# Where the operands of the matrix multiplications start in SBUF: weights at 0, moving activations at 192, stationary activations at 0, modulo 256 bytes

## The chip, the core and the metric

One core of a Trainium2 chip runs the whole program. The metric is the time of one execution on the device in microseconds (us). A core has TensorE (PE; its weight loads are listed apart, as PEld), VectorE (DVE), ScalarE (ACT), GpSimd (POOL) and SyncE (SP), which here issues the weight transfers.

## The reference

Two transformer blocks work on one sequence of 256 tokens of width 1024, all in float32.

```python
# first block
z = rms_norm(x, g_mix) @ w_in
x = x + (gate0 * y_pool + gate1 * y_nsa + gate2 * y_mem) @ w_o      # pooling, sparse attention, memory attention
x = x + peer_ffn(rms_norm(x, g_ffn), w_q, sub_keys, u, v)           # 16384 one-neuron experts, top 16 of each of 8 heads
x = rms_norm(x, g_final)
# second block, two layers: the mixer is mla in the first, fox in the second
h = h + 0.5 * swiglu(rms_norm(h), w_in, w_out)                      # d_ff 2816
h = h + mixer(rms_norm(h))
h = h + 0.5 * swiglu(rms_norm(h), w_in, w_out)
h = h + sigmoid(rms_norm(h) @ w_gate) * (p @ w_proj)
return rms_norm(h)
```

The kernel computes the product with all 16384 experts densely: `peer_u` is a 1024 x 16384 projection, `peer_v` a 16384 x 1024 one, and the top-16 gates are a mostly zero factor between them.

## The kernel before, in words

Every large weight comes in units of 128 partitions x 1024 columns (512 KB). `unit` (L243) gives each unit one DMA into a `raw` buffer (three of them), then a rounding copy on ACT into `hi` (L262, type float32r) and the remainder `lo = raw - hi` on DVE or POOL (L263). Activations are split in the same way. `mm3` (L279) makes one product of three matmuls from a stationary pair L and a moving pair R: L281 multiplies the hi of both, L282 the hi of L with the lo of R, L283 the lo of L with the hi of R.

There are two forms. In `ws_chunk` the weights are stationary (128 columns) and the activations X move past them, 256 tokens at a time: 8 steps of `mm3`, 24 matmuls for a unit. It is used for 20 units of `w_ws`, 16 of `peer_q`, 128 of `peer_u`, 176 of `ffn_in` and 16 of `fox_qk`: 356 units, 8544 matmuls. In the other form (`proj`, `go`, `cols_xs`) the activations are stationary and 512 columns of weights move: 12 matmuls for a unit. `peer_v` has 128 such units (1536 matmuls), `ffn_out` 88 (1056).

A matmul reads its moving operand from SBUF while the stationary operand of the next one is loaded, also from SBUF. Both run along the free dimension in every partition, so what can differ between two buffers is the byte address at which they start in the partition. The allocator rounds tiles up to 32 bytes and lays the tiles of a pool one behind the other. In the program before, the `raw` buffers begin at byte 18528 of the partition, the tiles that live across stages (`h0`, `h1`, `hThi`, ...) at 63936, and the tiles of each stage at 93952 = 367 x 256. This gives, modulo 256 bytes:

- `whi` (four buffers of 1032 floats = 4128 bytes): 192, 224, 0, 32; `wlo`: 64, 96, 128, 160. They are used as the pairs (192, 64), (224, 128), (0, 96), (32, 160).
- the `wx` places, where units go while attention buffers are free (the tiles of `qT`, `kT`, `v`, `Ohi`, `Olo` in the second block): 128 for hi and lo alike; the places in `U`, in the second half of `peer_v`: 0 for both.
- `hThi` and `hTlo`, the activations that move in most `ws_chunk` calls: 192; `Xhi` and `Xlo` of the second block (moving in `fox_qk`): 0.
- stationary activations: `W` and the upper part of `U` in `peer_v` 0, `ah` in `ffn_out` 128, `t2hi`/`t2lo` 32, `y4`/`Mt` 96, `Ohi`/`Olo` 128.

Two units are named below by their buffers: the unit that runs from 505.3 to 508.2 us lies in the pair (192, 64), and the one from 508.2 to 511.05 us in the pair (0, 96). The unit from 1509.8 to 1512.5 us lies in a `wx` place (128, 128). All three have X at 192.

The program is one fixed order for each engine: PE's order follows the Python loops and `weave`. `order` (L220) turns the four pairs and the places round. In the first part of `peer_u` the routing of tokens to experts (`routing`, L1020) runs on DVE beside it, and POOL makes every `lo`.

Of the kernel before, what the change touches and what calls it, by code (L numbers as in the profile page):

```python
# [9 lines left out]
F32 = mybir.dt.float32  # L10
F32R = mybir.dt.float32r
BF16 = mybir.dt.bfloat16
I32 = mybir.dt.int32
# [9 lines left out]
WU = 1032  # L23
# [115 lines left out]
N_G = 99  # L139
# [64 lines left out]
class Prog:  # L204
# [38 lines left out]
    def unit(self, src, w=1024, parts=1):  # L243

        nc = self.nc
        raw = self.strm.tile([128, WU], F32, name="raw", bufs=3)[:, :w]
        cuts = [slice(i * w // parts, (i + 1) * w // parts) for i in range(parts)]
        for c in cuts:
            nc.sync.dma_start(raw[:, c], src[:, c])
        self.n_unit += 1  # L250

        i = next(i for i in self.order if i < 0 or i in self.slots and w <= 1024)
        self.order.remove(i)
        self.order.append(i)
        if i >= 0:
            hi, lo = [v[:, :w] for v in self.slots[i]()]
        else:
            hi = self.strm.tile([128, WU], F32R, name="whi", bufs=4)[:, :w]
            lo = self.strm.tile([128, WU], F32R, name="wlo", bufs=4)[:, :w]
        e = nc.gpsimd if self.pool_lo and self.n_unit % self.pool_lo == 0 else nc.vector  # L260
        for c in cuts:
            nc.scalar.activation(hi[:, c], raw[:, c], AF.Copy)  # L262
            e.tensor_tensor(lo[:, c], raw[:, c], f32(hi[:, c]), op=OP.subtract)  # L263
        return hi, lo
# [147 lines left out]
    def run(self):  # L412
        nc, tc, a = self.nc, self.tc, self.a
        self.ones = self.const.tile([128, 1], F32, name="ones")
        nc.vector.memset(self.ones, 1.0)
        self.mhalf = self.const.tile([128, 1], F32, name="mhalf")

        nc.scalar.activation(self.mhalf, self.ones, AF.Copy, scale=-0.5)
        self.gc = self.const.tile([128, N_G], F32, name="gc")
        nc.sync.dma_start(self.gc, a["gcols"])  # L420
        i_ = self.const.tile([128, 128], I32, name="iota_i")
        nc.gpsimd.iota(i_, pattern=[[1, 128]], base=0, channel_multiplier=0)
        self.ident = self.const.tile([128, 128], F32, name="ident")
        nc.sync.dma_start(self.ident, a["c_ident"])
        self.io = self.const.tile([128, 128], F32, name="io")
        nc.vector.tensor_copy(self.io, i_)
        self.h = [self.res.tile([128, 1024], F32, name=f"h{t}") for t in range(2)]
        if WARM:

            z = self.h[0][:, :256].bitcast(BF16)  # L430
            nc.vector.memset(self.h[0][:, :256], 0.0)
            ps = self.mm()
            for _ in range(WARM):
                nc.tensor.matmul(ps, z[:, :128], z, start=True, stop=True)
        with ExitStack() as s:
            self.block1(s)
        if self.stop <= 1:
            return
        with ExitStack() as s:
            self.peer(s)  # L440
        if self.stop <= 2:
            return
        with ExitStack() as s:
            self.block2(s)
# [5 lines left out]
    def block1(self, s):  # L450
        nc, tc, a = self.nc, self.tc, self.a
        b1 = s.enter_context(tc.tile_pool(name="b1", bufs=1))
        self.junk = b1.tile([128, 1024], BF16, name="junk")

        turn = [0]
# [34 lines left out]
        X = N.X  # L490
# [38 lines left out]
        for t in range(2):  # L529
            n = 7 if t == 0 else 15  # L530
            ps = self.mm()
            for c in range(n):
                o = 128 - t * 128 + 16 * c + 31
# [43 lines left out]
        for c in "kv":  # L577
            w = b1.tile([128, 16, 64], F32, name="wcmp" + c, tag="pooled" if c == "k" else "uu")
# [75 lines left out]
        def cmp_scores(t):  # L654
            yield on("Ck", "sig", "q")
            ps = self.mm()
            for i in range(8):
                r, gp = divmod(i, 2)
                self.m32(ps[:, i * 32:(i + 1) * 32], qT[:, i, t * 128:(t + 1) * 128],
                         kcbd[:, gp].rearrange("p a b -> p (a b)"))  # L660
            sc = b1.tile([128, 16, 15], F32, name="sc")
            pr = b1.tile([128, 16, 32], F32, name="prc", tag="pr", bufs=4)
            st = b1.tile([128, 4, 16], F32, name="stc")
            nc.gpsimd.memset(pr, 0.0)
            nc.vector.tensor_tensor(sc.rearrange("p (g r) b -> p r g b", r=4),
                                    ps[:, :256].rearrange("p (r g b) -> p r g b", r=4, b=16)[:, :, :, :15],
                                    biasc[:, t].rearrange("p (g r) b -> p r g b", r=4), op=OP.add)
            nc.vector.tensor_reduce(st[:, 0], sc, axis=AX.X, op=OP.max)
            nc.vector.tensor_tensor(sc, sc, st[:, 0, :, None].to_broadcast([128, 16, 15]), op=OP.subtract)
            nc.scalar.activation(sc, sc, AF.Exp)  # L670
            nc.vector.tensor_reduce(st[:, 1], sc, axis=AX.X, op=OP.add)
            nc.vector.reciprocal(st[:, 2], st[:, 1])
            nc.vector.tensor_tensor(st[:, 3], st[:, 2], sig[:, t, 0], op=OP.mult)
            if t == 0:
                nc.vector.tensor_scalar(st[:, 3], st[:, 3], has, None, op0=OP.mult)
            nc.vector.tensor_tensor(pr[:, :, :15], sc, st[:, 3, :, None].to_broadcast([128, 16, 15]), op=OP.mult)
            yield 5.0
            pt = self.mm()
            for g in range(4):
                self.tpose(pt[:, g * 128:(g + 1) * 128], pr[:, 4 * g:4 * g + 4].rearrange("p r b -> p (r b)"))  # L680
            nc.scalar.activation(pct[:, t, :, ::-1], pt.rearrange("p (g q) -> p g q", g=4), AF.Copy)
            flag.add(f"pc{t}")
# [141 lines left out]

        kx = b1.tile([128, 4, 256], F32, name="kx")
        qx = b1.tile([128, 4, 256], F32, name="qx")
        vx = b1.tile([128, 2, 512], F32, name="vx")

        def memory():
            Nm = Norm(self, b1, self.gc[:, G_MEM:], x=(b1.tile([128, 8, 256], F32R, name="t2hi"),  # L830
# [125 lines left out]
    def peer(self, s):  # L956
        nc, tc, a = self.nc, self.tc, self.a
# [6 lines left out]
        X = N2.X  # L964
# [31 lines left out]
        for hp in range(16):  # L996
# [12 lines left out]
            if 4 <= hp < 12:  # L1009
                k = hp - 4  # L1010
# [4 lines left out]
            nc.scalar.activation(X[0][:, k], Hn[:, k], AF.Copy)  # L1015
            nc.vector.tensor_tensor(X[1][:, k], Hn[:, k], f32(X[0][:, k]), op=OP.subtract)  # L1016

        rt = self.res.tile([128, 1024], F32, name="rt")[:, :768].rearrange("p (i t) -> p i t", i=3)

        def routing(t):  # L1020
            o = 18432 if t == 0 else 30720
# [118 lines left out]
        for ip in range(64):  # L1140
# [4 lines left out]
            n = prog["tok"]  # L1145
# [28 lines left out]
                         tuple(u[j][:, h * 512:(h + 1) * 512] for j in range(2)), i == 0, i == 127)  # L1174

        gfin = self.res.tile([128, 1024], F32, name="gfin", tag="rt")
        gg = self.res.tile([128, 8], F32, name="gg")
        nc.vector.tensor_tensor(gg, self.gc[:, G_FIN:G_FIN + 8], self.gc[:, G_F2:G_F2 + 8], op=OP.mult)
        for i in range(128):
            if i == 64:  # L1180
# [17 lines left out]
        self.N3 = N3 = Norm(self, self.res, gg, x=self.hT(),  # L1198
                                 y=lambda: view(next(ys), 512))
        ss = N3.ss  # L1200
        r1 = self.res.tile([128, 2], F32, name="r1")

        self.junk = view(12288, 512, BF16)
        s2 = self.res.tile([128, 2, 2], F32, name="s2")
# [31 lines left out]
    def block2(self, s):  # L1236
        nc, tc, a = self.nc, self.tc, self.a
# [13 lines left out]
        turn = [0]  # L1251

        def next_norm(g):
            turn[0] ^= 1
            X = (tuple(b2.tile([128, 8, 256], F32R, name="X" + c) for c in ("hi", "lo")) if turn[0] else self.hT())
            return Norm(self, b2, self.gc[:, g:], x=X, y=ny)

        def res_stage(N, scale=None):
# [507 lines left out]
```

## Time and profile before

| | us |
|---|---|
| median of 3 runs | 2249.47 (2247.63 to 2249.92) |
| the profiled execution | 2250.61 |
| its span, first to last instruction | 2248.8 |
| PE busy | 2194.7 (98%) |
| DVE busy | 1505.9 (67%) |
| ACT busy | 1094.4 (49%) |
| POOL busy | 164.3 (7%) |
| DMA, mean busy share of 16 engines | about 50% |

The page gives one execution. "mean ns" of a matmul runs from its start to its modelled end, and neighbours overlap: PE starts the next one before that end. How often PE starts one is read from a stretch in which it does nothing else: length through count. Times inside the trace are counted from the first instruction.

### The profile page before, as it was taken

The numbers are of one execution on the slowest core, as the hardware profiler recorded it, in microseconds if no ns is written. First come the engines' busy times: TensorE is split into PE (matmuls) and PEld (weight loads), VectorE is DVE, ScalarE is ACT, GpSimd is POOL, SyncE is SP. The second block draws the span as 40 slices with busy tenths as digits, with TensorE's granted clock in tenths as the row PEclk, the third lists the DMA queues.
The fourth block names the chain that finished last, engine by engine and source line by source line (L and its number), as shares of the span: only waits on it lengthen the run. The fifth ranks groups of instructions, "written<-read, shape, count | busy, mean of one in ns | idle before, by whom it ended". The sixth has DMA issues, their size and how long they took to land. (4 is left out here: it accounts for less than half of the span.)

```text
span 2248.8 us, 37085 instructions
## 1 busy us (share of the span) xinstructions
PE 2194.7 (98%) x14402; PEld 1980.8 (88%) x14402; DVE 1505.9 (67%) x3071; ACT 1094.4 (49%) x1739; POOL 164.3 (7%) x141
## 2 busy tenths in 40 slices
PE   6999999999999999999999999999999999999998
PEld 5987788899999998888887999889998999989996
DVE  6656557998888985566565754865556655675555
ACT  3356544455444444455544543654445544554445
POOL 5000000284000000000001000100001000000000
PEclk7999999999999999999999999999999999999999
DMA  5632255455444456556554754445554653555553
GB/s 183 202 132 76 85 179 195 132 187 168 148 148 150 150 174 204 190 190 216 190 193 133 232 190 147 135 149 189 187 169 149 224 189 124 187 170 187 187 183 104
DMA packets 105171, 378.18 MB, mean 168 GB/s; under 512 B 12089, under 2 KB 12273, under 8 KB 104738
## 3 DMA queue, kind: packets, MB, share of 16 engines
q1 hardware_dynamic: 102832, 369.24, 50.0%
q0 software_dynamic: 1920, 6.37, 0.9%
q8 instruction: 113, 1.85, 0.3%
q14 instruction: 64, 0.52, 0.1%
q10 hardware_dynamic: 242, 0.20, 0.0%
HBM read 373.62 MB, written 2.14 MB: 167 GB/s over the span
## 5 line engine op out<-in xcount | busy, mean ns | idle before, releaser
L262 ACT ACTIVATE whi<-raw 128x1024 fp32r<-128x1024 f32 (+3 forms) x527 | 551.2, 1047 | 534.2 <-PE mm L282 347.6
L263 DVE TENSOR_TENSOR wlo<-raw,whi 128x1024 fp32r<-128x1024 f32 (+3 forms) x493 | 598.4, 1217 | 285.7 <-ACT whi L262 284.9
L281 PE MATMUL mm<-hThi,whi 128*128 128x256 f32 x2080 | 593.6, 286 | 22.9 <-ACT hThi L304 13.8
L282 PE MATMUL mm<-hTlo,whi 128*128 128x256 f32 x2080 | 589.9, 284 | 4.0 <-DVE hTlo L1016 2.7
L283 PE MATMUL mm<-hThi,wlo 128*128 128x256 f32 x2080 | 586.8, 282 | 1.2 <-DVE wlo L263 1.2
L281 PEld LDWEIGHTS mm<-hThi,whi 128*128 128x128 f32 x2080 | 394.6, 190 | 28.6 <-ACT hThi L304 14.0
L282 PEld LDWEIGHTS mm<-hTlo,whi 128*128 128x128 f32 x2080 | 396.2, 191 | 8.1 <-DVE hTlo L1016 2.9
L283 PEld LDWEIGHTS mm<-hThi,wlo 128*128 128x128 f32 x2080 | 395.4, 190 | 2.1 <-DVE wlo L263 2.1
L263 DVE TENSOR_TENSOR wx<-raw,wx 128x1024 fp32r<-128x1024 f32 x140 | 173.4, 1239 | 107.1 <-ACT wx L262 107.0
L262 ACT ACTIVATE wx<-raw 128x1024 fp32r<-128x1024 f32 x140 | 147.7, 1056 | 135.7 <-PE mm L283 95.2
L281 PE MATMUL mm<-hThi,wx 128*128 128x256 f32 x640 | 179.3, 281 | 2.4 <-ACT hThi L164 2.4
L282 PE MATMUL mm<-hTlo,wx 128*128 128x256 f32 x640 | 179.5, 281 | 0.3 <-DVE hTlo L165 0.3
L283 PE MATMUL mm<-hThi,wx 128*128 128x256 f32 x640 | 179.2, 280 | 0.0
L281 PEld LDWEIGHTS mm<-hThi,wx 128*128 128x128 f32 x640 | 120.6, 189 | 4.1 <-ACT hThi L164 2.8
L282 PEld LDWEIGHTS mm<-hTlo,wx 128*128 128x128 f32 x640 | 120.7, 189 | 1.7 <-issue 0.5
L283 PEld LDWEIGHTS mm<-hThi,wx 128*128 128x128 f32 x640 | 121.0, 189 | 0.0
L1103 DVE TENSOR_SCALAR h<-io,rt 128x128 f32<-128x128 f32 x256 | 93.7, 366 | 22.2 <-PE mm L273 21.9
L281 PE MATMUL acc<-whi,W 128*128 128x512 f32 x256 | 101.0, 395 | 0.0
L283 PE MATMUL acc<-whi,W 128*128 128x512 f32 x256 | 101.0, 394 | 0.0
L282 PE MATMUL acc<-wlo,W 128*128 128x512 f32 x256 | 100.8, 394 | 0.0
L263 POOL TENSOR_TENSOR wlo<-raw,whi 128x1024 fp32r<-128x1024 f32 x34 | 85.1, 2510 | 68.0 <-ACT whi L262 66.2
L1304 ACT ACTIVATE ah<-sg 128x256 fp32r<-128x256 f32 x88 | 36.6, 416 | 97.8 <-DVE sg L1301 97.8
(497 smaller groups left out, 4053.9 us busy)
## 6 DMA issues: line engine op xcount, KB each, us to landing
raw<-in_ffn_in SPq DMA_DIRECT2D x176, 512.0 KB, 3.7
raw<-in_peer_u SPq DMA_DIRECT2D x128, 512.0 KB, 3.8
raw<-in_peer_v SPq DMA_DIRECT2D x128, 512.0 KB, 3.5
raw<-in_ffn_out SPq DMA_DIRECT2D x88, 512.0 KB, 3.6
raw<-in_w_mrg SPq DMA_DIRECT2D x24, 512.0 KB, 3.5
raw<-in_w_ws SPq DMA_DIRECT2D x19, 512.0 KB, 4.2
raw<-in_w_peer_q SPq DMA_DIRECT2D x16, 512.0 KB, 4.3
raw<-in_ple_g SPq DMA_DIRECT2D x16, 512.0 KB, 3.5
```

The source lines that it names most:

```text
L262: nc.scalar.activation(hi[:, c], raw[:, c], AF.Copy)
L263: e.tensor_tensor(lo[:, c], raw[:, c], f32(hi[:, c]), op=OP.subtract)
L281: m(ps, L[0], R[0], start=first, stop=False, skip_group_check=True)
L282: m(ps, L[0], R[1], start=False, stop=False, skip_group_check=True)
L283: m(ps, L[1], R[0], start=False, stop=last, skip_group_check=True)
L1103: nc.vector.tensor_scalar(A[:, j], self.io, i1, g, op0=OP.is_equal, op1=OP.mult)
L1304: nc.scalar.activation(hi, sg, AF.Copy)
```

## The change

It changes where tiles start and what they are padded to. No arithmetic changes, and `mm3`, its callers and the order of the units stay.

- `unit`: the separate tiles `whi` and `wlo` become one tile `w2` of 2112 floats (8448 bytes, 33 x 256), four buffers as before; hi starts at float 0, lo at float 1024 (at 1056 for the wide units of `fox_v`).
- the constants `iota_i` and `io` (512 bytes each) leave the constant pool; `io` now lies in free columns of `rt`, and `iota` on POOL with its copy on DVE is issued in `peer` just ahead of the routing. `gc` is padded from 99 to 115 columns.
- `gg` is taken first in its pool and padded to 192 bytes, `r1` padded to 64; the first block's `stc` and `vx` are padded; `Xhi` and `Xlo` become tiles of 2112 and 2144 floats of which columns 48 to 2096 are used.

```diff
@@ unit
-            hi = self.strm.tile([128, WU], F32R, name="whi", bufs=4)[:, :w]
-            lo = self.strm.tile([128, WU], F32R, name="wlo", bufs=4)[:, :w]
+            pair = self.strm.tile([128, 2112], F32R, name="w2", bufs=4)
+            o = 1024 if w <= 1024 else 1056
+            hi, lo = pair[:, :w], pair[:, o:o + w]
@@ run
-        self.gc = self.const.tile([128, N_G], F32, name="gc")
-        nc.sync.dma_start(self.gc, a["gcols"])
-        i_ = self.const.tile([128, 128], I32, name="iota_i")
-        nc.gpsimd.iota(i_, pattern=[[1, 128]], base=0, channel_multiplier=0)
+
+        self.gg = self.res.tile([128, 48], F32, name="gg")[:, :8]
+        self.h = [self.res.tile([128, 1024], F32, name=f"h{t}") for t in range(2)]
+        self.gc = self.const.tile([128, N_G + 16], F32, name="gc")
+        nc.sync.dma_start(self.gc[:, :N_G], a["gcols"])
         self.ident = self.const.tile([128, 128], F32, name="ident")
         nc.sync.dma_start(self.ident, a["c_ident"])
-        self.io = self.const.tile([128, 128], F32, name="io")
-        nc.vector.tensor_copy(self.io, i_)
-        self.h = [self.res.tile([128, 1024], F32, name=f"h{t}") for t in range(2)]
@@ block1
-            st = b1.tile([128, 4, 16], F32, name="stc")
+            st = b1.tile([128, 112], F32, name="stc")[:, :64].rearrange("p (a b) -> p a b", a=4)
...
-        vx = b1.tile([128, 2, 512], F32, name="vx")
+        vx = b1.tile([128, 1080], F32, name="vx")[:, :1024].rearrange("p (t d) -> p t d", t=2)
@@ peer
-        rt = self.res.tile([128, 1024], F32, name="rt")[:, :768].rearrange("p (i t) -> p i t", i=3)
+        rt = self.res.tile([128, 1024], F32, name="rt")
+        self.io = rt[:, 768:896]
+        rt = rt[:, :768].rearrange("p (i t) -> p i t", i=3)
+        i_ = view(20480 - 128, 128, I32)
+        nc.gpsimd.iota(i_, pattern=[[1, 128]], base=0, channel_multiplier=0)
+        nc.vector.tensor_copy(self.io, i_)
...
-        gg = self.res.tile([128, 8], F32, name="gg")
+        gg = self.gg
...
-        r1 = self.res.tile([128, 2], F32, name="r1")
+        r1 = self.res.tile([128, 16], F32, name="r1")[:, :2]
@@ block2
-            X = (tuple(b2.tile([128, 8, 256], F32R, name="X" + c) for c in ("hi", "lo")) if turn[0] else self.hT())
+            X = (tuple(b2.tile([128, n], F32R, name="X" + c)[:, 48:2096].rearrange("p (k t) -> p k t", k=8)
+                       for c, n in (("hi", 2112), ("lo", 2144))) if turn[0] else self.hT())
```

## Rows read from the trace of the kernel before

**Rows 1.** The page: its span and PE's line.

```profile
span 2248.8 us, 37085 instructions
PE 2194.7 (98%) x14402; PEld 1980.8 (88%) x14402; DVE 1505.9 (67%) x3071; ACT 1094.4 (49%) x1739; POOL 164.3 (7%) x141
```

**Rows 2.** PE's waits, longest in total first: total us, times, longest.

```profile
PE mm L281 <- ACT hThi L304: 13.8, 1, 13.8
PE mm L281 <- ACT hThi L164: 8.6, 4, 2.6
```

**Rows 3.** Windows: busy us and instructions of each engine, clock, DMA share, GB/s.

```profile
core 0: us, PE busy (x) PEld busy (x) DVE busy (x) ACT busy (x) POOL busy (x), PEclk, DMA share, GB/s
...
500.00:535.00 35.00, 35.00 (x297) 35.00 (x296) 34.96 (x59) 18.11 (x21) 27.02 (x12) 1.00 0.53 176
560.00:820.00 260.00, 260.00 (x2223) 260.00 (x2222) 227.31 (x661) 117.66 (x203) 0.00 (x0) 1.00 0.46 151
870.00:1035.00 165.00, 165.00 (x712) 133.28 (x711) 99.70 (x126) 83.44 (x128) 0.00 (x0) 1.00 0.57 190
...
1260.00:1380.00 120.00, 119.84 (x855) 112.44 (x854) 73.10 (x90) 57.13 (x76) 0.00 (x0) 1.00 0.62 202
1509.77:1512.49 2.72, 2.72 (x26) 2.72 (x25) 2.39 (x3) 1.06 (x1) 0.00 (x0) 1.00 0.66 229
```

**Rows 4.** Groups by line within 500 to 535 us: count, busy us, mean ns.

```profile
L281 PE MATMUL mm<-hThi,whi 128*128 128x256 f32 x99 | 27.8, 281 | 0.0
```

**Rows 5.** Groups by line within 870 to 1035 us.

```profile
L282 PE MATMUL acc<-wlo,W 128*128 128x512 f32 x237 | 93.3, 394 | 0.0
```

**Rows 6.** Single lines, 509.28 to 511.04 us: count, ns min/median/max, first and last start.

```profile
L281 PE MATMUL mm<-hThi,whi x5: 277/277/277, 509.3 to 510.7; 128*128 128x256 f32 x5
L282 PE MATMUL mm<-hTlo,whi x6: 285/285/286, 509.0 to 510.8; 128*128 128x256 f32 x6
L283 PE MATMUL mm<-hThi,wlo x6: 278/279/279, 509.2 to 510.9; 128*128 128x256 f32 x6
```

**Rows 7.** The same for one line, 506.45 to 508.2 us.

```profile
L281 PE MATMUL mm<-hThi,whi x5: 278/282/285, 506.4 to 507.9; 128*128 128x256 f32 x5
```

**Rows 8.** The same for one line, 1509.9 to 1512.25 us.

```profile
L281 PE MATMUL mm<-hThi,wx x8: 276/276/276, 1509.8 to 1512.1; 128*128 128x256 f32 x8
```

**Rows 9.** The same for one line, 508.22 to 508.5 us.

```profile
L281 PE MATMUL mm<-hThi,whi x1: 287/287/287, 508.2 to 508.2; 128*128 128x256 f32 x1
```

**Rows 10.** Groups by line within 1260 to 1380 us.

```profile
L282 PE MATMUL mm<-hTlo,wx 128*128 128x256 f32 x120 | 33.5, 279 | 0.0
```

**Rows 11.** Single lines, 1060 to 1185 us, units in the places of U.

```profile
L281 PE MATMUL acc<-U x78: 389/389/398, 1064.9 to 1184.4; 128*128 128x512 f32 x78
L282 PE MATMUL acc<-U x78: 387/389/389, 1065.1 to 1184.6; 128*128 128x512 f32 x78
```

**Rows 12.** Groups by line over the whole span.

```profile
L282 PE MATMUL mm<-hTlo,wx 128*128 128x256 f32 x640 | 179.5, 281 | 0.3 <-DVE hTlo L165 0.3
L282 PE MATMUL acc<-wx,ah 128*128 128x512 f32 x184 | 71.9, 391 | 0.0
L282 PE MATMUL acc<-wlo,ah 128*128 128x512 f32 x168 | 66.5, 396 | 0.0
L283 PE MATMUL acc<-whi,y 128*128 128x512 f32 x32 | 13.0, 407 | 0.0
```

**Rows 13.** Groups by line within 10 to 100 us.

```profile
L281 PE MATMUL mm<-hThi,whi 128*128 128x256 f32 x125 | 36.4, 291 | 13.8 <-ACT hThi L304 13.8
```

**Rows 14.** POOL by line, 424 to 520 us, and the timeline at the start.

```profile
L263 POOL TENSOR_TENSOR wlo<-raw,whi 128x1024 fp32r<-128x1024 f32 x29 | 73.0, 2525 | 66.8 <-ACT whi L262 65.1 <-PE mm L281 1.5
0.84 0.24 POOL L422 IOTA iota_i<- 128x128 int32 x1 [0.40 <-POOLq L1758]
```

**Rows 15.** Timelines of DVE and PE where the second routing ends.

```profile
531.28 2.47 DVE L1104 TENSOR_SCALAR h<-io,rt 128x128 f32<-128x128 f32 x1
539.51 0.49 PE L287 MATMUL mm<-ident,R 128*128 128x128 f32 x3
```

## The prediction

> **What bounds the kernel now.** I read the page first: of the span of 2248.8 us PE is busy 2194.7 [rows 1], and PE's waits are short: the longest is 13.8 us, once, at the start, and the next group 8.6 us in total [rows 2]. So the time is what PE's stream takes. Then I read stretches in which PE does one thing [rows 3]. From 870 to 1035 us it starts 712 matmuls of 512 columns, two of them reaching in from the left: 165 / 710 = 232.4 ns each; their mean duration is 394 ns [rows 5]. From 500 to 535 us, matmuls of 256 columns: 35 / 295 = 118.6 ns, with durations of 281 ns and a little over [rows 4]. In both, start to start is the duration less 162 to 163 ns, so a duration in ns tells the pace of one matmul to a nanosecond: pace = duration - 162.5.
>
> Next, what the pace depends on. In the unit from 508.2 to 511.05 us (weights at 0 and 96, X at 192) the three lines settle at 277, 285 and 279 ns, the same at nearly every step [rows 6]. While L281 runs, hi is loaded once more (at 0, for L282); while L282 runs, lo (at 96, for L283); while L283 runs, hi (at 0). So a moving operand that starts 192 bytes after the one being loaded, modulo 256, goes with 277 to 279 ns (114.5 to 116.5 of pace), one 96 after it with 285 (122.5). The unit before it (192 and 64) wavers between 278 and 285 on one line [rows 7]. The fastest pace is in the unit at 1509.8 us: 276 ns at every step [rows 8], and as a check 2.72 us for 24 starts, 113.3 ns [rows 3]. Other units in such places have 279 on average [rows 10]. For 512 columns the best rows are in U, where weights and stationary operand both start at 0: 389 ns [rows 11], against 394 beside it. So the pace of one and the same matmul differs by 2 to 8% with where its operands lie and how it falls in with its neighbours, and the clock is 1.00 in all these stretches, its upper level of 2.4 GHz.
>
> **The change part by part.** Where things end up: the constant pool loses 1024 bytes and gains 64, so raw begins at 17568 and the pairs at 17568 + 3 x 4128 = 29952 = 117 x 256. Each is 33 x 256 long: hi and lo at 0 in all four. They end at 63744, gg takes 192, and h0 begins at 63936 as before: hThi and hTlo stay at 192. In the second block Xhi and Xlo get 192 by their 48 columns, and the two are 640 bytes longer, which moves ah, wx, Ohi, Olo from 128 to 0. In the first, the pads move t2 and y4 to 0. So 256-column matmuls get the distance 192 throughout, and 512-column ones 0, except where X itself is stationary (gates, fox_v, mla_down, ple_g: distance 64; I give these nothing).
>
> 256 columns, weights in the four pairs: of 8544 matmuls in 356 units 3 x 640 = 1920 are in wx [rows 12], which leaves 6624. In the first 100 us PE waits for its transfers; the 3 x 125 there [rows 13] I count at nothing. 6250 remain, at 281.3 ns. For the new pace the bounds are 276, the lowest row [rows 8], and 281.3, no gain; I take 277, which the distance 192 shows in the row nearest to the new state: hi loaded after hi, both at 0 [rows 6]. 6250 x 4.3 ns = 26.9 us. In wx: 1920 x (279.3 - 277) = 4.4 us.
>
> 512 columns: peer_v has 64 units x 12 = 768 matmuls with W at 394.3, which go to the 389.7 of the rows in U: 3.5 us. Of its second 64 units about 37 (four of seven places) lie in the pairs: 444 x 4.3 = 1.9 us. In ffn_out the pairs have 396 to 397 (504 matmuls), the places wx some 393 (552) although both their operands are at 128, distance 0 as well: entering from 256-column work costs something that the layout may leave. I take 391.5 for both: 504 x 5.5 = 2.8 and 552 x 1.5 = 0.8 us. Products with t2, y4, Mt, O stationary (some 528, 395 in clean stretches; single groups are at 407 with their waits [rows 12]): 528 x 3.5 = 1.8 us. Sum 10.8 us; the bounds are 0 and, at 389.5 everywhere, 15.
>
> What lies beside it. While POOL makes every lo, one takes 2525 ns [rows 14], and a unit of PE goes from 24 x 118.6 = 2.85 to 2.75 us: it still fits, with 0.2 us to spare. DVE is full until about 534 us (34.96 of 35 in [rows 3]). By 531 us it has left the routing for the gating (L1104), and PE reads the routing's result at 539.5 [rows 15], so PE could come 8 us earlier; at the new pace it comes 3 us earlier. In the gating that follows DVE is busy 227 of 260 us [rows 3], 87%; at the new pace about 90%. Since little is to spare in the routing, I take 3 us off for it. If that cover were gone altogether, the gain of peer_u (3072 x 4.3 = 13 us) would go. ACT and DMA are at 62% or less.
>
> The moved constants: iota takes 0.24 us on POOL [rows 14]; the copy on DVE I put at 0.3, by the other 128-column DVE operations in these rows without their waits. They now stand ahead of the routing on engines that wait for that stage's first tiles; nothing is queued behind them there but the routing, which starts 8 us ahead of need by the same rows. Between -0.3 (the start loses them) and +0.5 us: 0. The merged tile: hi's buffer now comes free with lo's, one matmul later (0.12 us) and four units ahead of need: 0. Pads: 0.
>
> The sum: 26.9 + 4.4 + 10.8 - 3 = 39.1 us. Against the profiled execution, 2250.6 - 39.1 = 2211.5; that one is 1.1 us above the median of the runs, so 2210 for the median.
>
> The Trainium skill, in "TensorE: Matmul & The Clock Gate", step 1 of Part 2, speaks against the change: PE has two independent SBUF read ports, and loading the next weights takes no read bandwidth from the running matmul. By that, layout would be worth nothing and the time stays 2249. The trace does not agree as far as the pace goes: 277 and 285 ns alternate in one unit whose matmuls differ in nothing but the operands' place [rows 6]. What is shared the trace does not tell; rival 2 reaches the same time from rows of this kernel.
>
> **The rivals.**
> 1. The pace is a matter of phase more than of distance. For: the same addresses (192, 128, 128) give 276 in one unit [rows 8] and 279 on average [rows 10]; and 277 + 285 + 279 makes 841, near 3 x 279 = 837, as if the credit of one line were paid by the next. Against: 277 stands in five steps running, always on the same line. Then all 256-column work settles at 279.3: 6250 x 2.0 = 12.5, plus 10.8 for the 512-column work: 23 us, 2226 us; with half of the 512-column gain and none for wx 2231.
> 2. Layout does nothing by itself: what looks like place is which engine writes beside it. By it each unit keeps its pace and the time is 2249. For: units in the pair (192, 64) waver [rows 7], which a fixed place would not. Against: [rows 6] and [rows 11], steady over whole units.
> 3. Slower: a bad phase that keeps itself up. The first L281 of the unit in [rows 6] has the favoured distance and takes 287 ns, 124.5 of pace [rows 9]. With every unit alike there is no neighbour of another class to knock the stream out of it. If all of it enters so and stays: 6250 x 5.7 + 1920 x 7.7 = 50 us, less 10.8: 2289. It is slower from the point where the mean of the 256-column work, now 280.8 over the two kinds, rises by more than 10.8 us / 8170 = 1.3 ns, above 282.1. Against: in that unit it is gone after three steps.
> 4. Another engine sets the end in peer_u: 13 - 3 = 10 us are lost, 2220.
>
> **How the numbers follow.** Forecast (a mean of 276 to 278 for 256 columns: 2202 to 2218) 0.70; rival 1 0.15; rival 2 0.06; rival 3 0.05; rival 4 0.04. The predicted time is 2210. The lower end: at 276 everywhere the 256-column term is 33.1 + 6.3 = 39.4, and the 512-column one at most 15: with the 3 us off, 51 us, 2198; I take 2199. The upper end takes in rivals 1 and 4: 2232. A measurement of this kernel tells about 0.2%, 4.5 us, from no change. Faster by more than that: 0.70 + 0.15 + 0.04 = 0.89; within it: rival 2, 0.06; slower: rival 3, 0.05.
>
> **What would show it.** In the changed profile L281, L282 and L283 of the 256-column groups should all have a mean near 277, without the 285 on L282; 870 to 1035 us (now earlier) should have about 390 for all three lines with W; windows of pure 256-column work should give 114.5 ns a matmul. PE's waits should stay as they are. If the means are 279 and mixed, it is rival 1; unchanged means, rival 2; a mean over 282.1, rival 3; new waits of PE for DVE or POOL between 445 and 820 us, rival 4. The forecast is wrong if the distance that looks good in one line out of three does not stay good when all three have it.

## The result, and the profile after

| | before | changed |
|---|---|---|
| median | 2247.76 us (6 runs, 2245.53 to 2249.92) | 2221.61 us (6 runs, 2218.53 to 2230.61) |
| profiled execution | 2250.61 us | 2221.97 us |
| its span | 2248.8 us | 2220.2 us |

The ratio is 0.989, with an interval of 0.987 to 0.991: 26 us faster. The forecast was 2210, the range 2199 to 2232. The direction held, and the size is two thirds of the forecast. Of the mechanism, the part on matmuls of 512 columns held, and the part on those of 256 columns held in some stretches only.

The source has one more line ahead of `mm3` now, so L281, L282 and L283 of before are L282, L283 and L284, and the tiles `whi` and `wlo` are both called `w`. The page of the changed kernel, its span and PE's line (before: [rows 1]):

```profile
span 2220.2 us, 37112 instructions
PE 2162.3 (97%) x14402; PEld 1960.8 (88%) x14402; DVE 1500.5 (68%) x3071; ACT 1093.9 (49%) x1739; POOL 169.0 (8%) x141
```

PE still sets the time. The windows that answer to [rows 3] (busy us and count of PE, PEld, DVE, ACT, POOL; clock; DMA share; GB/s):

```profile
500.00:535.00 35.00, 32.65 (x285) 32.21 (x284) 30.78 (x47) 17.04 (x20) 24.13 (x10) 1.00 0.52 171
560.00:820.00 260.00, 260.00 (x2299) 260.00 (x2298) 232.16 (x677) 120.73 (x210) 0.00 (x0) 1.00 0.48 157
870.00:1035.00 165.00, 165.00 (x730) 136.62 (x729) 103.17 (x129) 86.18 (x128) 0.00 (x0) 1.00 0.61 198
```

In the 260 us of peer_u's second part PE starts 2299 matmuls instead of 2223, in the 165 us of peer_v 730 instead of 712. In the 35 us of the routing it is idle for 2.35 us, which it was not before. The groups by line tell where the pace changed and where it didn't. First peer_u, 560 to 820 us (count, busy us, mean ns):

```profile
L283 PE MATMUL mm<-hTlo,w 128*128 128x256 f32 x614 | 169.6, 276 | 0.0
```

Then peer_v, 870 to 1030 us (before: [rows 5]), all three lines at the 389 that only the places in U had before [rows 11]:

```profile
L283 PE MATMUL acc<-w,W 128*128 128x512 f32 x226 | 87.9, 389 | 0.0
...
L282 PE MATMUL acc<-w,W 128*128 128x512 f32 x225 | 87.5, 389 | 0.0
```

And an ffn stage, 1265 to 1345 us (before: 279 for wx [rows 10], 280 to 283 for the pairs):

```profile
L283 PE MATMUL mm<-hTlo,wx 128*128 128x256 f32 x78 | 21.9, 281 | 0.0
...
L284 PE MATMUL mm<-hThi,w 128*128 128x256 f32 x72 | 20.2, 281 | 0.0
L282 PE MATMUL acc<-wx,ah 128*128 128x512 f32 x28 | 10.9, 389 | 0.0
```

So the 512-column work went to its best pace everywhere, the 256-column work of peer_u too (276, below the forecast's 277), but that of ffn_in, of the same form and at the same distance of 192, sits at 281. It does so in all four ffn stages, and it isn't a mixture: single lines of the two stretches (min, median, max; first and last start; the weight loads are the PEld lines) show two paces with nothing in between. Peer_u, 620 to 625 us:

```profile
L284 PE MATMUL mm<-hThi,w x14: 276/276/277, 619.9 to 624.3; 128*128 128x256 f32 x14
L284 PEld LDWEIGHTS mm<-hThi,w x13: 187/188/188, 620.1 to 624.2; 128*128 128x128 f32 x13
```

An ffn stage, 1302.7 to 1308.4 us:

```profile
L284 PEld LDWEIGHTS mm<-hThi,w x16: 192/192/192, 1302.9 to 1308.2; 128*128 128x128 f32 x16
L284 PE MATMUL mm<-hThi,w x16: 281/281/281, 1303.0 to 1308.3; 128*128 128x256 f32 x16
```

Start to start that is 113.3 and 117.8 ns. At the slower of the two paces the weight load itself is recorded 4 ns longer, at an unchanged place.

Summed over the trace, from each matmul's start to the next one's: where no wait falls in and the step isn't the entry into a run (200 ns and more), the 256-column step has a mean of 118.1 ns before (8484 of them) and 115.7 after, which is 8484 x 2.4 = 20.4 us; the 512-column step 231.3 (3596) and 227.6, 13.3 us. The spans differ by 28.6 us, so 5.1 us came back as waits and clock.

### The profile page after: what moved, and what is told of

It reads as the page before. It is cut to its first block, busy times and chain, and to the rows that moved or that the text cites. A ratio compares the mean times of both kernels' runs of the same rounds, so it can differ in the third digit from the quotient of the medians.

```text
span 2220.2 us, 37112 instructions
## 1 busy us (share of the span) xinstructions
PE 2162.3 (97%) x14402; PEld 1960.8 (88%) x14402; DVE 1500.5 (68%) x3071; ACT 1093.9 (49%) x1739; POOL 169.0 (8%) x141
## 5 line engine op out<-in xcount | busy, mean ns | idle before, releaser
L264 DVE TENSOR_TENSOR w<-raw,w 128x1024 fp32r<-128x1024 f32 (+3 forms) x493 | 597.8, 1217 | 283.5 <-ACT w L263 282.5
L263 ACT ACTIVATE w<-raw 128x1024 fp32r<-128x1024 f32 (+3 forms) x527 | 551.9, 1049 | 446.9 <-PE mm L284 246.4
L282 PE MATMUL mm<-hThi,w 128*128 128x256 f32 x2080 | 589.7, 284 | 25.7 <-ACT hThi L305 12.8
L284 PE MATMUL mm<-hThi,w 128*128 128x256 f32 x2080 | 582.9, 280 | 3.1 <-POOL w L264 2.0
L283 PE MATMUL mm<-hTlo,w 128*128 128x256 f32 x2080 | 583.4, 281 | 1.9 <-DVE hTlo L165 1.2
L282 PEld LDWEIGHTS mm<-hThi,w 128*128 128x128 f32 x2080 | 395.1, 190 | 31.8 <-ACT hThi L305 13.1
L284 PEld LDWEIGHTS mm<-hThi,w 128*128 128x128 f32 x2080 | 397.8, 191 | 4.1 <-POOL w L264 2.2
L283 PEld LDWEIGHTS mm<-hTlo,w 128*128 128x128 f32 x2080 | 395.5, 190 | 5.5 <-issue 2.3
L263 ACT ACTIVATE wx<-raw 128x1024 fp32r<-128x1024 f32 x140 | 147.9, 1056 | 129.8 <-PE mm L284 86.2
L282 PE MATMUL mm<-hThi,wx 128*128 128x256 f32 x640 | 180.0, 282 | 2.4 <-ACT hThi L164 2.4
L283 PE MATMUL mm<-hTlo,wx 128*128 128x256 f32 x640 | 180.6, 282 | 0.3 <-DVE hTlo L165 0.3
L284 PE MATMUL mm<-hThi,wx 128*128 128x256 f32 x640 | 180.4, 282 | 0.0
L282 PEld LDWEIGHTS mm<-hThi,wx 128*128 128x128 f32 x640 | 120.6, 189 | 4.0 <-ACT hThi L164 2.8
L284 PEld LDWEIGHTS mm<-hThi,wx 128*128 128x128 f32 x640 | 123.3, 193 | 0.0
L283 PEld LDWEIGHTS mm<-hTlo,wx 128*128 128x128 f32 x640 | 121.0, 189 | 1.7 <-issue 0.5
L1107 DVE TENSOR_SCALAR h<-rt 128x128 f32<-128x128 f32 x256 | 92.2, 360 | 11.4 <-PE mm L274 11.2
L283 PE MATMUL acc<-w,W 128*128 128x512 f32 x256 | 99.6, 389 | 0.0
L282 PE MATMUL acc<-w,W 128*128 128x512 f32 x256 | 99.6, 389 | 0.0
L284 PE MATMUL acc<-w,W 128*128 128x512 f32 x256 | 99.6, 389 | 0.0
L264 POOL TENSOR_TENSOR w<-raw,w 128x1024 fp32r<-128x1024 f32 x34 | 87.0, 2575 | 64.3 <-ACT w L263 63.0
```

Source lines behind the costliest of these rows:

```text
L282: m(ps, L[0], R[0], start=first, stop=False, skip_group_check=True)
L283: m(ps, L[0], R[1], start=False, stop=False, skip_group_check=True)
L284: m(ps, L[1], R[0], start=False, stop=last, skip_group_check=True)
L1107: nc.vector.tensor_scalar(A[:, j], self.io, i1, g, op0=OP.is_equal, op1=OP.mult)
```

## The experiments

All are edits of the changed kernel but one. Theory A (the prediction's): the pace goes by the distance from the loading operand to the moving one, and 192 is good. Theory B: any layout that is the same for all units has a good and a bad pace, and entry alone chooses.

**Other distances for the pairs.** The pairs are moved inside their tiles; X stays at 192.

```diff
-            o = 1024 if w <= 1024 else 1056
-            hi, lo = pair[:, :w], pair[:, o:o + w]
+            h, o = (32, 1056) if w <= 1024 else (0, 1056)     # both at 128: distance 64 (these notes aren't in the code)
+            hi, lo = pair[:, h:h + w], pair[:, o:o + w]
...
+            h, o = (48, 1072) ...    # both at 192: distance 0
+            h, o = (24, 1048) ...    # both at 96: distance 96
+            h, o = (0, 1048) ...     # hi at 0, lo at 96: distances 192, 96, 192 while L282, L283, L284 run
```

Pairs at 128:

> The changed kernel with the four weight pairs 128 bytes further on (hi and lo both at 128 modulo 256, X still at 192, so the distance of the 256-column work in the pairs is 64; the wx places and everything else as in the changed kernel). Theory A, the distance decides and 192 is the good one: the 256-column matmuls of peer_u fall back to 279 to 281 ns mean (117 to 118.5 ns of pace) from the 276 of the changed kernel, and the time is about 3072 x 4.3 ns = 13 us longer, with some 3 us more for peer_v, whose weights now move 128 past a stationary operand at 0: 2238 us. Theory B, phase: every uniform layout has a fast pace (113.3 ns) and a slow one (117.7 ns), and what PE did just before a stretch chooses between them; peer_u, which PE enters after a gap, stays at 276 ns, ffn_in, which it enters straight from 512-column work, stays at 281, and only peer_v is slower: 2225 us.

Pairs at 192:

> The same with the pairs 192 bytes further on: distance 0 for the 256-column work in the pairs, and in peer_v weights at 192 moving past a stationary operand at 0. Theory A: peer_u at 280 to 282 ns mean (the units of the kernel before with hi at 192 were at 119 ns), 13 us and some 3 us for peer_v longer: 2238 us. Theory B: peer_u stays at 276 ns, 2225 us.

Pairs at 96:

> The same with the pairs 96 bytes further on: distance 96 for the 256-column work in the pairs, the distance that went with 285 ns in the kernel before. Theory A: peer_u at 285 ns on all three lines, 122.5 ns of pace, 3072 x 9 = 28 us longer, the pairs' share of ffn_in another 2304 x 4 = 9 us: about 2260 us. Theory B: peer_u at 276 ns, 2225 us.

hi at 0, lo at 96:

> The changed kernel with lo alone 96 bytes further on: hi at 0 and lo at 96 in all four pairs, as in one of the four pairs of the kernel before. Theory A: each line goes by the distance of what is loaded beside it, so the three lines stand at 277, 285 and 279 ns throughout peer_u (mean 280.3) and the time is about 13 us longer than the changed kernel's, 2235 us. Theory B: a mixture cannot hold the fast pace; the mean is the same 280, but the first steps of a unit do not differ from the last, and it does not matter which line has 96.

Measured, one execution each: 2245.44, 2259.06, 2257.05 and 2238.95 us, beside 2245.74 for the kernel before (A had 2238, 2238, 2260 and 2235; B 2225 for the first three). Groups by line, 560 to 820 us, with the pairs at 128, and under it at 192, at 96, and at 0 and 96:

```profile
L283 PE MATMUL mm<-hTlo,w 128*128 128x256 f32 x598 | 167.4, 280 | 0.0
L284 PE MATMUL mm<-hThi,w 128*128 128x256 f32 x598 | 166.9, 279 | 0.0
```

```profile
L284 PE MATMUL mm<-hThi,w 128*128 128x256 f32 x587 | 166.0, 283 | 0.0
```

```profile
L284 PE MATMUL mm<-hThi,w 128*128 128x256 f32 x588 | 166.1, 283 | 0.0
L283 PE MATMUL mm<-hTlo,w 128*128 128x256 f32 x587 | 164.5, 280 | 0.0
```

```profile
L283 PE MATMUL mm<-hTlo,w 128*128 128x256 f32 x592 | 168.6, 285 | 0.0
L284 PE MATMUL mm<-hThi,w 128*128 128x256 f32 x592 | 165.2, 279 | 0.0
```

What follows: B said 276 in peer_u for every uniform layout, and none of them settles there. The distances 0 and 96 are slower than both paces of the changed kernel, 119.8 and 120.0 ns a step on average in this window, so layout does something by itself. The last kernel has the pattern of [rows 6] throughout (285 on the line in whose time lo is loaded from 96). But A's sizes were off: a uniform distance of 96 costs 120.0 ns a step on average, not 122.5. There too steps of 120 to 125 ns on some lines stand beside steps of 115 to 119 on others, so what one line shows in [rows 6] isn't the price of its distance alone. And the 512 columns need the pairs at 0 too: peer_v's three lines stood at 395 with the pairs at 128, at 396, 396 and 395 with the pairs at 192, and at 392 to 399 with the pairs at 96.

That 192 is better than 64 for 256 columns is not shown. With the pairs at 128 this window has 2233 starts, 117.8 ns a step, and in the second profiled execution of the changed kernel (further down) it has 2233 as well. The fast pace occurs with the pairs at 128 too, for the ten us ahead of 500 us. The window, and that line:

```profile
560.00:820.00 260.00, 260.00 (x2233) 260.00 (x2232) 227.28 (x663) 117.92 (x204) 0.00 (x0) 1.00 0.47 151
L283 PE MATMUL mm<-hTlo,w x29: 276/276/279, 490.1 to 500.0; 128*128 128x256 f32 x29
```

The 17 us by which its span exceeds that of the second execution (2243.7 against 2226.4) lie elsewhere: by the starts of the same matmuls 6.4 up to 512 us, 7.1 from 860 to 1195 (peer_v), and 0.1 from 536 to 860.

X stayed at 192 in these four, so they don't part the distance from the place of the weights. A stretch of the changed kernel does. In the first block t2 moves from 0 past weights at 0: 96 matmuls at the distance 0, which the prediction counted among those at 192. Their step is 119.7 ns on average in both executions, as with the pairs and X both at 192. So the distance 0 is slow in both places. One of the three lines:

```profile
L283 PE MATMUL mm<-t2lo,w x32: 280/283/283, 101.7 to 117.5; 128*128 128x256 f32 x32
```

What A doesn't explain is ffn_in. It differs from peer_u in its entry: each of its runs of 48 matmuls follows a 512-column matmul without a gap. The timeline of the changed kernel (start us, us, engine, line):

```profile
1302.53 0.39 PE L284 MATMUL acc<-wx,ah 128*128 128x512 f32 x1
1302.76 0.28 PE L282 MATMUL mm<-hThi,w 128*128 128x256 f32 x1
```

The next run begins at 1311.13, so one cycle of 48 and 12 matmuls takes 8.37 us. From here on the theory is A': the distance permits 113.3 ns, and the entry decides whether a run gets it.

**A short matmul ahead of each ffn_in run.** Once of float32r and 64 columns, once of float32 and 16; the next product overwrites its result.

```diff
+                    nc.tensor.matmul(pg[:, :64], us[0][0][:, :128], X[0][:, 0, :64], start=True, stop=True,
+                                     skip_group_check=True)
```

64 columns:

> The changed kernel with one more matmul ahead of each run of 48 matmuls of ffn_in but the first (a product of 64 float32r columns whose result the next one overwrites), so that 256-column work no longer follows 512-column work directly. Theory A' (at the distance 192 there are two paces, 113.3 and 117.7 ns, and the way in which a run is entered chooses): at least part of ffn_in falls from 281 to 276 ns; if all of it does, 4224 x 4.3 = 18 us less some 80 x 0.1 = 8 us for the added matmuls, about 2212; ffn_in at 276 is what tells. Rival C (ffn_in is at 281 for what runs beside it, its transfers or its writes, whatever the entry): 281 stays, and the time is 2222 plus 8, about 2230.

16 columns of float32 (`self.ident` and `self.ident[:, :16]` in its place):

> As the one with 64 columns, but the added matmul is of type float32 (16 columns of the identity), which is what stands ahead of the fast runs in peer_u. Theory A': 276 ns in ffn_in, 18 us less some 80 x 0.15 = 12 us, about 2215; if this one does it and the one with 64 columns doesn't, the kind of entry matters and not only that 512 and 256 columns are parted. Rival C: 281 stays, about 2234.

Measured: 2228.94 and 2253.52 us, beside 2250.66 for the kernel before and 2228.19 for the changed one. Groups of the first, 1265 to 1345 us, and then of the second:

```profile
L283 PE MATMUL mm<-hTlo,w 128*128 128x256 f32 x88 | 24.3, 276 | 0.0
L283 PE MATMUL mm<-hTlo,wx 128*128 128x256 f32 x72 | 19.9, 276 | 0.0
L1301 PE MATMUL mm<-hThi,w 128*128 128x64 f32 x6 | 1.2, 192 | 0.0
```

```profile
L283 PE MATMUL mm<-hTlo,w 128*128 128x256 f32 x80 | 22.5, 281 | 0.0
...
L283 PE MATMUL mm<-hTlo,wx 128*128 128x256 f32 x72 | 20.2, 281 | 0.0
```

What follows: with 64 columns all ffn_in runs at 276, in pairs and wx alike; rival C (it is what runs beside it) falls. With the other it stays at 281, a miss of A', though the two kinds are parted there as well: a gap alone is not what opens the fast pace. Its cycle is 8.63 us instead of 8.37, and 84 x 0.26 = 22 us of its 25 us over the repeated changed kernel are that. For the first the time doesn't follow. A cycle is 8.31 us in the trace, 60 ns less, since the short matmul takes back most of the 48 x 4.5 = 216 ns; that is some 5 us in all, and this execution had lost 3.9 us on the repeated changed kernel before the first ffn stage (its peer_u fell to 281 a little earlier, and its window 500 to 535 has a clock of 0.95 for 1.00).

**The routing spread thinner, and the changed kernel once more.**

```diff
-PA,PB,SA,SB=1,0,8,3
+PA,PB,SA,SB=1,0,7,3
```

> The changed kernel with one number changed: in peer_u the routing is spread so that its DVE work is issued for 7 instead of 8 units of its schedule. Theory A' with rival 4 of the prediction (the waits of PE for ACT and POOL from 504 to 507 us come from the routing beside it): PE's waits there shrink by 2 to 5 us, and the time is 2217 to 2220. If they come from something else: 2222, or more where the routing now ends too late.

The changed kernel again:

> The changed kernel once more, unaltered, beside the three others. Theory A': its peer_u at 276 and its ffn_in at 281 ns again, since the entries are the same in every execution; 2219 to 2227. Rival C says the same of the means. If stretches change their pace from one execution to the next, the choice is not made by the program's order alone, and single differences under 8 us between kernels are not to be read.

Measured: 2230.11 and 2228.19 us. The spread routing gives PE its 35 us back:

```profile
500.00:535.00 35.00, 35.00 (x306) 34.82 (x304) 35.00 (x46) 17.04 (x20) 27.93 (x13) 1.00 0.52 176
560.00:820.00 260.00, 260.00 (x2233) 260.00 (x2232) 226.94 (x666) 117.53 (x206) 0.00 (x0) 1.00 0.47 152
```

but no time comes of it, because its peer_u runs at 281 from 560 us on. The repeated kernel tells why that is no effect of the edit. Its windows, and a line from 620 to 625 us:

```profile
500.00:535.00 35.00, 33.01 (x288) 32.76 (x288) 32.22 (x43) 17.77 (x21) 23.93 (x10) 1.00 0.54 180
560.00:820.00 260.00, 260.00 (x2233) 260.00 (x2232) 227.92 (x671) 117.59 (x205) 0.00 (x0) 1.00 0.46 151
```

```profile
L284 PE MATMUL mm<-hThi,w x14: 281/281/281, 620.1 to 624.7; 128*128 128x256 f32 x14
```

The same program, and 2233 starts instead of 2299. The expectation that peer_u would be at 276 again was a miss. From 511 to 535 us both executions are at 113.3; then they part. The timeline of the profiled execution of the changed kernel, and under it that of the repeat:

```profile
535.55 1.17 PE L274 MATMUL mm<-h,h 128*128 128x128 f32 x9
537.30 0.39 PE L282 MATMUL mm<-hThi,w 128*128 128x256 f32 x1 [0.58 <-ACT R L1160]
```

```profile
535.03 1.06 PE L274 MATMUL mm<-h,h 128*128 128x128 f32 x8
535.86 0.39 PE L282 MATMUL mm<-hThi,w 128*128 128x256 f32 x1
```

In the one PE waits 0.58 us ahead of a run and goes on with steps of 222, 120, 117, 116, 114, 113 ns; in the other it enters without a wait, with 221, 119, 117, 118, 118, and keeps 117.8 through more than 2000 matmuls to the end of peer_u, over the float32 products between the runs as well (each later run is entered with a first step of 206 ns in the one and 200 in the other). 66 starts x 113 ns = 7.5 us is what it makes of this window, and the two times lie 6.2 us apart. That fits the six times of the changed kernel: four from 2218.5 to 2222.0 and two at 2226.8 and 2230.6; those have no trace, so it is not shown for them. In the traces the slow pace is the commoner: the four other kernels that leave peer_u as it is (both with an added matmul, and below the one with the cut and the one with four cuts) all have 2233 starts in this window.

The idle PE at 504 to 507 us costs some 2 us: by the starts the kernel with the spread routing gains 2.1 us on the repeat from 500 to 512 us. But it had lost 1.8 us from 440 to 500 us, where its step is 117.8 ns and that of the repeat 114.3 on average, so the two times don't show it.

**The 512-column matmul cut in two.** The last of the 512-column matmuls ahead of a run is cut into 448 + 64 columns: a short matmul without added work.

```diff
+        if cut:
+            m(ps[:, :cut], L[1], R[0][:, :cut], start=False, stop=last, skip_group_check=True)
+            m(ps[:, cut:], L[1], R[0][:, cut:], start=False, stop=last, skip_group_check=True)
...
-                    go(1, m, u)
+                    go(1, m, u, cut=448)
```

> The changed kernel in which the last 512-column matmul ahead of each ffn_in run is cut into one of 448 and one of 64 columns, so that the short matmul stands between the two kinds without being added work. In the kernel with an added 64-column matmul ffn_in ran at 277 instead of 281 ns. Theory A' (the distance allows 113.3 ns, and how a run is entered decides whether it gets it): ffn_in at 277 ns again, 88 runs x 43 x 4.3 ns = 16 us, less 84 x 0.11 us = 9 us for the load that the short matmul can't hide and the settling behind it: about 7 us under the changed kernel, 2213 to 2221 as peer_u comes out at 276 or 281. Rival D (the added matmul helped by its weights, those of the next product, not by its length): ffn_in stays at 281, and the time is that of the changed kernel plus 2 to 9 us.

The same, and in peer_u's second part a 64-column matmul ahead of every fourth pair of units, one in 27 us, eleven in all ("every second pair", 11 us and 12 in the expectation are slips):

> As the kernel with the cut matmul, and in the gating part of peer_u a 64-column matmul ahead of every second pair of units (about one in 11 us). Theory A': peer_u from 560 us on is at 276 ns in every execution instead of in some; against an execution that has 281 there it is 2233 to 2299 starts in 260 us, 10 us less some 12 x 0.12 = 1.4 us; the times of the executions lie within 3 us of each other, about 2212. Rival D, or a state that the fp32 products between the runs set anew each time: peer_u is mixed, and the spread stays as in the changed kernel, some 10 us.

The same cut in the kernel before, with its own layout (its hi at 224 has the distance 224, not 32):

> The kernel before, in its own layout, with the same cut matmuls ahead of the ffn_in runs. Theory A': the short matmul lets in the fast pace only where the distance bears it; the pairs (distances 0, 160, 192, 32 for hi) keep a mean of 281 and more, the time is 2249 plus 0 to 9 us, and 276 appears at most in the wx places (distance 64). Rival E (the way of entry alone makes the pace, the layout of weights and activations matters for nothing but the 512 columns): ffn_in falls to 277 in the old layout too, and the time to about 2242.

Measured: 2225.75 us (2221.49 to 2229.85, 4 runs; ratio 0.9891, 0.9875 to 0.9908), 2219.25 us (2217.84 to 2229.67, 5 runs; 0.9867, 0.985 to 0.9883), and 2256.02 us, beside 2248.35. Groups of the first, 1265 to 1345 us; the window of peer_u of the second; groups of the third, 1265 to 1345 us:

```profile
L283 PE MATMUL mm<-hTlo,w 128*128 128x256 f32 x81 | 22.4, 276 | 0.0
L283 PE MATMUL mm<-hTlo,wx 128*128 128x256 f32 x72 | 19.9, 276 | 0.0
```

```profile
560.00:820.00 260.00, 260.00 (x2297) 260.00 (x2297) 232.34 (x684) 120.11 (x209) 0.00 (x0) 1.00 0.48 155
```

```profile
L282 PE MATMUL mm<-hTlo,wx 128*128 128x256 f32 x77 | 21.5, 279 | 0.0
...
L282 PE MATMUL mm<-hTlo,whi 128*128 128x256 f32 x72 | 20.3, 282 | 0.0
```

What follows. Rival D falls: the length matters, not whose weights it has. Rival E falls: in the old layout the same entry leaves 279 to 282 and only costs, so the new layout and the new entry are both needed. In the second kernel peer_u is at 276 (2297 starts), but that isn't the work of its short matmuls: it is at 276 from its first run at 541.4 us on, and the first of them starts at 561.3 us. A line of peer_u ahead of them, and they themselves:

```profile
L283 PE MATMUL mm<-hTlo,w x48: 276/276/281, 541.6 to 560.3; 128*128 128x256 f32 x48
L1154 PE MATMUL mm<-hThi,w x11: 192/277/277, 561.3 to 832.6; 128*128 128x64 f32 x11
```

So whether they hold peer_u at 276 in every execution is not shown. Four of its five times lie within 2.2 us; the fifth, the profiled one, is 10 us longer with peer_u at 276 as well. Its mean granted clock is 0.983, that of the four 0.987 to 0.990: 0.0055 x 2228 = 12 us by an estimate, so the clock can account for it.

The gain that A' promised for the first isn't in its times, and its peer_u is at 281 (2233 starts). Eleven of its short matmuls, one for each cycle, start from 1262.2 to 1344.9 us: 8.27 us a cycle, 0.1 us less; over 84 runs that is 8 us. Its profiled execution gave them back in three stretches: by the starts it takes 1.9 us longer than the repeated changed kernel from 1621 to 1711 us, 2.5 from there to 1784, and 2.3 from 2174 to 2219 us; its clock is 0.95 from 1700 to 1720 us and 0.91 from 2180 to 2200, that of the other 1.00 in both. In the second stretch PE waits for ACT's `ah`, where the repeat waits 0.2 us:

```profile
1739.17 0.50 PE L282 MATMUL acc<-wx,ah 128*128 128x512 f32 x1 [2.22 <-ACT ah L1313]
```

Whether the cut makes the clock fall there is open: the profiled execution is the longest of the four.

**Four ways to cut.** One for each ffn stage: 384 + 128, 320 + 192, 256 + 256, 352 + 160.

```diff
+CUT = (384, 320, 256, 352)
...
-                    go(1, m, u, cut=448)
+                    go(1, m, u, cut=CUT[j])
```

> The kernel with the cut matmul, with another cut in each of the four ffn stages: the last 512-column matmul ahead of an ffn_in run is cut into 384 + 128, 320 + 192, 256 + 256 and 352 + 160 columns, in the order of the stages. A cycle of an ffn stage (48 matmuls of 256 columns, 12 of 512) takes 8.373 us in the changed kernel, at 281 ns, and 8.273 with 448 + 64, at 276. Theory A'' (a matmul too short to hide the next load lets in the fast pace, and the load that sticks out is its price, some 90 of the 185 ns gained): the longer the second part, the smaller the price, until the whole load is hidden and the entry is that of the uncut one again; so 256 + 256 stays at 281 and 8.373, and 192 and 160 columns, if they still break the entry, give 8.19 to 8.25. Rival F (any change of the length ahead of the run will do, the load plays no part): 256 + 256 gives 276 too, and a cycle of 8.373 - 0.185 = 8.19 us.

Measured: 2227.59 us, beside 2248.72, with peer_u at 281 (2233 starts). The second parts of the cut matmuls, by stage (one for each cycle; first and last start):

```profile
L287 PE MATMUL acc<-w,ah x6: 250/250/250, 1525.0 to 1592.2; 128*128 128x192 f32 x6
L287 PE MATMUL acc<-wx,ah x4: 250/250/250, 1516.6 to 1575.4; 128*128 128x192 f32 x4
...
L287 PE MATMUL acc<-wx,ah x8: 282/282/283, 1744.3 to 1826.3; 128*128 128x256 f32 x8
L287 PE MATMUL acc<-w,ah x4: 282/282/283, 1760.7 to 1834.5; 128*128 128x256 f32 x4
```

The 192-column stage has ten in 75.6 us, 8.40 us for a cycle; the 256-column one twelve in 90.2 us, 8.20. In the same way 128 columns give 8.25 and 160 columns 8.22, both at 276. What follows: with 192 columns ffn_in stays at 281, and with 256 + 256 it is at 276. Groups from 1520 to 1600 us and, under it, from 1760 to 1840 us:

```profile
L289 PE MATMUL mm<-hThi,wx 128*128 128x256 f32 x72 | 20.2, 281 | 0.0
```

```profile
L284 PE MATMUL mm<-hTlo,w 128*128 128x256 f32 x80 | 22.1, 277 | 0.0
L289 PE MATMUL mm<-hThi,wx 128*128 128x256 f32 x80 | 22.1, 276 | 0.0
```

That is what rival F said, and A'' falls: it isn't a weight load that sticks out which opens the fast pace, since 192 columns leave it shut and 256, which start on time (steps of 113 and 119 ns), open it. The price was as A'' said, though: nothing sticks out with 256 + 256, so nearly the whole gain stays, 8.37 - 8.20 = 0.17 us a cycle. It is the cut to try: over 88 cycles 15 us, an estimate, as a kernel with it in all four stages wasn't run. Part of that may come back: the cycle ahead of those twelve took 11.35 us, with PE waiting 2.1 us in it for ACT's `ah`.

## Why the prediction was right, and where it was off

- **What bounds the kernel, and the pace by duration:** held. PE is busy 97% of the span, and every gain is one of start-to-start time. That layout does something (against rival 2) is settled by the runs: with PE, its instructions and their order the same, the pairs at 0, 128, 192 and 96 give 2222 (2228 in the repeat), 2245, 2259 and 2257 us. The Trainium skill's rule in "TensorE: Matmul & The Clock Gate", step 1 of Part 2 (two independent read ports, no bandwidth taken from the running matmul) is not what this kernel's traces show as far as the pace goes: in peer_u 113.4 or 117.8 ns a step with the pairs at 0 against 119.8 with the pairs at 192. What is shared they don't tell.
- **512 columns, 10.8 us forecast:** 13.3 us by the mean steps. The 389 of the places in U [rows 11] is what all of this work got, ffn_out included, for which I had taken 391.5 with a cost of entry. There is such a cost only behind fast runs (in the kernel with 448 + 64 steps of 232, 233, 230 ns and then 227).
- **256 columns, 26.9 + 4.4 us forecast:** this term failed. It measured 20.4 us in the profiled execution and, by 117.0 instead of 115.7 ns, 8484 x 1.1 = 9.3 us in the repeat. The step was "I take 277, which the distance 192 shows in the row nearest to the new state", for all 8170 matmuls. At that distance there are two paces, 113.3 and 117.8 ns, and how the stream comes to a run decides which it keeps. In peer_u it got the first, better than forecast (276), in the profiled execution. That was luck: in the repeat and the four other traces with the same peer_u it got the second, and 3072 x (118.5 - 117.8) = 2 us came of it instead of 13. What the layout alone gives 256 columns is nearer to the 9.3 us of the repeat. In ffn_in it got the second: 4224 matmuls, of which I expected 4.4 + 2304 x 4.3 ns = 14.3 us, gave 4224 x (118.1 - 117.8) = 1.3. The 13.0 us between the two, less 2.5 gained beyond the forecast in the 512-column work and some 3 in peer_u (3072 x 1 ns), plus the 2.1 us by which the waits below exceed theirs, make 9.6 of the 10.5 us by which the profiled execution missed its forecast. Two readings were off besides: 96 of these matmuls, those in which t2 moves, got the distance 0 and not 192, and the 285 of [rows 6] is not what the distance 96 costs when all lines have it.
- **Rivals 1 and 3** had that mechanism between them. Rival 1 called it phase, as a mean for all; rival 3 described a bad phase that keeps itself up when no unit of another class knocks it out, and priced it by the one step of 287 ns [rows 9]. It does keep itself up, over 2000 matmuls, but at 281. I had the evidence, a unit at 276 and others at 279 in the same places [rows 8, 10], and put it down to a rival as if it excluded the distance. Both are needed: the old layout with the new entry stays at 279 to 282, the new layout with the old entry at 281. That it must be the distance 192 isn't shown: no other uniform layout was run with the new entry.
- **The routing, 3 us off:** right in kind, small in size. Against the mean steps 5.1 us came back in the profiled execution and 0.6 in the repeat, where peer_u is slower. PE now waits in the routing, on the work of POOL and ACT on hi and lo, which rival 4 gave as a sign:

```profile
504.72 0.38 PE L282 MATMUL mm<-hThi,w 128*128 128x256 f32 x1 [0.36 <-ACT w L263]
...
507.21 0.39 PE L284 MATMUL mm<-hThi,w 128*128 128x256 f32 x1 [1.99 <-POOL w L264]
```

  The 10 us of rival 4 didn't come: behind it peer_u went on at the fast pace in the profiled execution, and in the repeat PE is busy for all of 560 to 820 us, at the slow one.
- **Moved iota, merged tile, pads at nothing:** nothing in the waits or groups speaks against it; they weren't tried one by one.

## What to carry to other kernels

Where PE's stream is the time, read the start-to-start steps of one form of matmul: if the same form has several paces, look at where its stationary and moving operands start modulo 256 bytes, and try the few uniform layouts on the chip. A pace that one row shows is what the layout permits, not what every stretch will get: look at how each run of matmuls is entered, and price the stretches apart. Profile the same program twice before laying a pace to an edit: here one window had 2299 starts in one execution and 2233 in the next. And cutting the last long matmul ahead of a run of short ones into two halves can cost next to nothing and change the pace of the whole run; a shorter time for a whole kernel hasn't been shown from it yet.

## What was not expected of the hardware

- A stream of 256-column matmuls of one layout has two paces that keep themselves up, 113.3 and 117.8 ns (durations 276 and 281), with weight loads of 188 and 192 ns. The choice falls in the first five or six steps. They occur at the distance 64 as well (pairs at 128). What the phase is a phase of, the traces don't show.
- Ahead of ffn_in, second parts of 64, 128, 160 and 256 columns lead to 276, none and 192 columns to 281.
- The choice in peer_u differs between executions of the same program and is worth some 6 to 8 us. A wait ahead of the run doesn't decide it alone: one execution took the fast pace behind a wait of 0.58 us, the kernel with short matmuls in peer_u took it at 541.4 us without one.
- At the distance 0 a step takes 119.7 to 120.0 ns, with the weights and the moving operand both at 0 and both at 192.
